# Low parts of streamed weights: a negated copy on ScalarE and an accumulating load, in place of VectorE's subtraction

## The chip, the core and the metric

One core of a Trainium2 chip runs the whole program. The metric is the device time of one execution in microseconds (us). TensorE multiplies matrices, VectorE and ScalarE work on elements, GpSimd does some element work and issues its own DMAs, and SyncE issues most of the loads. In the profile they are PE (with PEld for its weight loads), DVE, ACT, POOL and SP.

## The reference, cut to what matters

One layer of a diffusion backbone in float32: 512 latent tokens and 256 context tokens of width 1024. Every heavy step is a product of activations with a weight matrix that is used once.

```python
def swiglu(x, w_in, w_out):
    a, b = jnp.split(x @ w_in, 2, axis=-1)
    return (jax.nn.silu(a) * b) @ w_out
...
h = h + 0.5 * g1 * swiglu(modulate(h, norm_ffn1[layer], sh1, sc1), w_ffn1_in[layer], w_ffn1_out[layer])
hc = hc + 0.5 * g1c * swiglu(modulate(hc, norm_ffn1[layer], sh1c, sc1c), w_ffn1_in[layer], w_ffn1_out[layer])
...
q, k, v, rg, cv, ga, gb = jnp.split(u @ w_in[layer], IN_SPLITS, axis=-1)
o, _, _ = bidir_retention(q, k, v, log_gf, log_gb, rf, rb)
h = h + g2 * mixer_output(o, rg, cv, ga, gb, *branch_w)
h = h + 0.5 * g3 * swiglu(modulate(h, norm_ffn2[layer], sh3, sc3), w_ffn2_in[layer], w_ffn2_out[layer])
return rmsnorm(h, final_norm)
```

`modulate` is an RMS norm with a scale and a shift per channel; these come from a product of a conditioning vector with `w_mod`. `mixer_output` joins a four-head retention and a convolution of width 31 by sigmoid gates. The SwiGLU's inner width is 2816.

## The kernel before, in words

The activations lie with channels on the 128 partitions and tokens along the free dimension. TensorE multiplies in the type float32r, which holds fewer bits than float32, so each operand is held as two float32r parts: a high part (the value rounded) and a low part (what the rounding took away). A product of two such pairs takes three matmuls (`mm3`, L90 to L92): high times high, high times the activation's low part, and, last, the weight's low part times the activation's high part.

Weights are streamed in 248 units of 128 partitions by 1024 columns (896 in some of the SwiGLUs' second matrices). `unit` (L77 to L84) makes one: SyncE loads the raw float32 tile (L79), ScalarE copies it into a float32r tile `wh` (L81), and VectorE subtracts that from the raw tile into `wl` (L83). Raw tiles, `wh` and `wl` have four buffers each, so the cast of a unit waits until TensorE has read the unit four earlier for the last time. `units` makes two at a time. The raw buffers (tag `wraw`) also serve the 56 tiles of `w_mod` that are streamed beside the first SwiGLU (`mods`, L175 to L185), the distance tables of the heads (L549), and the reloads of the retention's partial sums in the gates' stage (L759 to L761).

The order of the stages: the first modulations and norms with the first products (`start`, to about 80 us), the first SwiGLU for latent and context tokens, keys, queries, values, scores and gates of four heads with the convolution's chunks between them (`retention`, `conv_chunk`), the gates of the two branches with the convolution's layernorm, the projection and the merge, and the second SwiGLU. A SwiGLU's last four units are held together, and their products are taken for the first half of the tokens and then for the second, so that the next norm can begin early; the merge's last products do the same.

A planner lists the instructions of each engine in one order, by priority and by the time at which it reckons them ready; on the chip each engine runs its list in that order, and a wait at the head holds up the rest. GpSimd's list holds, beside 16 products at the start (L164): the stores of h (L437), the zeroed margins of the convolution's input (L503, L504, with two buffers), the stores of the retention's partial sums (L718), their reloads (L761) and the reload of h (L788). The 30 taps of a convolution chunk (L515) run on VectorE at a lowered priority.

In the changed kernel the cast stands at L82, the negated copy at L84 and the accumulating load at L85, one line down for the rest of the function.

Of the kernel before, what the change touches and what calls it, by code (L numbers as in the profile page):

```python
# [16 lines left out]
P = 128  # L17
# [12 lines left out]
EPS = 1e-6  # L30
# [7 lines left out]
CONV_AT = ((0, 1, 2), (3, 4), (5, 6), (7,))  # L38
# The modulations that are computed beside the first SwiGLU: (which of the nine, channel block).
MOD_STEPS = (  # L40
# [9 lines left out]
def hybrid_layer_kernel(ctx: ExitStack, tc: tile.TileContext, a: dict, out: bass.AP):  # L50
# [21 lines left out]

# [1 line left out]
    def raw_tile(shape):  # L74
        return t_(shape, F32, "wraw", 4)

    def unit(src, n=1024):  # L77
        raw = raw_tile((P, n))
        nc.sync.dma_start(raw, src)  # L79
        hi = t_((P, n), F32R, "wh", 4)  # L80
        nc.scalar.copy(hi, raw)  # L81
        lo = t_((P, n), F32R, "wl", 4)  # L82
        nc.vector.tensor_sub(lo, raw, f32(hi))  # L83
        return hi, lo  # L84
# [12 lines left out]
    def proj(o, w, xs, ks=None, c=slice(None)):  # L97
        """o += w.T @ xs for the blocks ks of the contraction, all by default."""
        n = len(xs)
        for k in range(n) if ks is None else ks:  # L100
            mm3(o, col(w, k), (xs[k][0][:, c], xs[k][1][:, c]), k == 0, k == n - 1)

# [1 line left out]
    cs = cp.tile([P, KT, 2], F32, name="cs")  # L104
# [22 lines left out]
    nc.scalar.activation(cs, cs, AF.Silu)  # L127
    # the rows of c and c_ctx on every partition
    first = t_((P, P), F32, "sc")
# [15 lines left out]
    def first_mods(b):  # L145
        """The first scale and shift of channel block b. The engines share the work: the tensor engine finds
        the scales, the vector engine the latent tokens' shift, GpSimd (with ScalarE's sums) the context's."""
        raw = [[t_((P, 512), F32, rtags[(4 * b + 2 * i + n) % 24]) for n in range(2)] for i in range(2)]
        for i in range(2):
            for n in range(2):  # L150
                nc.sync.dma_start(raw[i][n], a["w_mod0"][2 * b + i, :, n * 512:(n + 1) * 512])
        pm = ps()
        for k in range(KT):
            nc.tensor.matmul(pm[0:2, 0:P], cs[:, k, :], raw[0][k // 4][:, k % 4 * P:(k % 4 + 1) * P],
                             start=k == 0, stop=k == KT - 1)
        row = tmp()
        nc.vector.tensor_copy(row[0:2, 0:P], pm[0:2, 0:P])
        nc.tensor.transpose(pm[:, P:P + 2], row[0:2, 0:P], ident[0:2, 0:2])
        for n in range(2):
            c = slice(n * 512, (n + 1) * 512)  # L160
            nc.vector.scalar_tensor_tensor(tmp((P, 512), BF16), raw[1][n], 1.0, ccrow[0][:, c], ALU.mult, ALU.mult,
                                           accum_out=dots[:, b, 0, n:n + 1])
            m = tmp()
            nc.gpsimd.tensor_mul(m, raw[1][n], ccrow[1][:, c])  # L164
            nc.scalar.activation(m, m, AF.Copy, accum_out=dots[:, b, 1, n:n + 1])
        nc.vector.tensor_scalar(ab1[:, 0, b, :], pm[:, P:P + 2], bm1[:, 8 + b:9 + b], vec[:, V_N1 + b:V_N1 + b + 1],
                                ALU.add, ALU.mult)
        shift(slice(b, b + 1), 0)
# [21 lines left out]
    def scale_shift(key, src, sc, sh, nrm, b, n=1):  # L190
        """The per-channel factor w * (1 + scale) and the shift of a modulated norm, n blocks from b."""
        if key not in deriv:
            deriv[key] = cp.tile([P, 2, 8], F32, name=f"ab_{key}")
        t = deriv[key][:, :, b:b + n]
        j = 8 * sc + b
        nc.vector.tensor_add(t[:, 0, :], src[:, j:j + n], bm1[:, j:j + n])
        nc.vector.tensor_mul(t[:, 0, :], t[:, 0, :], vec[:, nrm + b:nrm + b + n])
        j = 8 * sh + b
        nc.vector.tensor_add(t[:, 1, :], src[:, j:j + n], vec[:, V_BM + j:V_BM + j + n])
# [12 lines left out]

# [1 line left out]
    def square_sum(acc, src, b):  # L214
        """Adds the squares of block b to acc; those of the last block stay apart."""
        if b == 0:
            nc.scalar.activation(acc, src, AF.Square)
            return None
        sq = tmp()[:, :src.shape[-1]]
        if b == KT - 1:  # L220
            nc.vector.tensor_mul(sq, src, src)
            return sq
        nc.scalar.activation(sq, src, AF.Square)
        nc.vector.tensor_add(acc, acc, sq)

    def rstd_sum(acc, sq, c):
        """1 / sqrt(mean + eps) of acc's and sq's sum over the channels, a diagonal block for 128 tokens each."""
        n = c.stop - c.start
        nt = n // P
        pv = ps()  # L230
        for i in range(nt):
            o = pv[:, 2 * i:2 * i + 2]
            nc.tensor.matmul(o, acc[:, c.start + i * P:c.start + (i + 1) * P], ones[:, 0:2], start=True, stop=False)  # L233
            nc.tensor.matmul(o, sq[:, i * P:(i + 1) * P], ones[:, 0:2], start=False, stop=True)  # L234
        v = tmp((P, 2, 4))
        y = v[:, 1, :nt]
        rsqrt(y, v[:, 0, :nt], pv[:, 0:2 * nt:2], 1.0 / D)
        dg = tmp()
        for i in range(nt):
            nc.vector.tensor_scalar_mul(dg[:, i * P:(i + 1) * P], ident_h, y[:, i:i + 1])  # L240
        return dg[:, :n]

    def rstd_bcast(dg):
        """The same factors on every partition, in PSUM."""
        pr = ps()
# [7 lines left out]
    def rsqrt(y, var, src, scale):  # L253
        """y = -2 / sqrt(var), with var = scale * src + EPS: the table's root and one of Newton's steps."""
        n = y.shape[-1]
# [31 lines left out]

# [1 line left out]
    def ffn(w_in, w_out, u, uc, tags, evac, evac_c, extra, head, tail):  # L289
        """head gives the products of the first two chunks; tail is called between the products of the last  # L290
        four units, which take the first half of the tokens before the second."""
        g, gc = [], []
# [59 lines left out]

# [1 line left out]
    whole, wholec = slice(0, L), slice(0, LC)  # L354
    u, uc = u_tiles(), uc_tiles()

    def start():
        """The first modulations and norms, and the first two chunks' products as their inputs come."""
        for b in range(KT):
# [104 lines left out]

    # log decays of both directions: min(z, 0) - log1p(exp(-|z|))
    lg = cp.tile([P, 8], F32, name="lg")
# [16 lines left out]

# [1 line left out]
    uc, u = st["uc"], st["u"]  # L485
# [34 lines left out]
    def roped(p, half, hi, lo):  # L520
        """Rotation of a block whose partitions are (x1, x2), by angles that run with the grid's
        rows (half 0) or columns (half 1)."""
        if half == 0:
# [14 lines left out]
    def windows(strip, off, n):  # L538
        """Two windows of a strip, 128 apart."""
        w = strip[:, off:off + n]  # L540
        return bass.AP(w.tensor, w.offset, [list(w.ap[0]), [P, 2], [1, n]])

    def strips(hd):
        """Decays of all distances, latent keys and context keys, for one head."""
        gf, gb = lg[:, hd:hd + 1], lg[:, 4 + hd:5 + hd]
# [17 lines left out]
    def retention(hd):  # L563
# [35 lines left out]
        if hd == 0:  # L599
            # the norm of the latent tokens ends beside the first products  # L600
            w = units(a["w_k"][hd])
# [15 lines left out]
        def values():  # L617
            """Values, with tokens on the partitions."""
            pv = [ps() for _ in range(6)]
# [22 lines left out]

        # scores of six key blocks, times the decays, for half of the queries at a time
        for nh in range(2):
# [77 lines left out]

# [1 line left out]
    ret, gcv, z = [], [], []  # L724
# [48 lines left out]

# [1 line left out]
    mg = u_tiles()  # L775
# [37 lines left out]

# [1 line left out]
    acc3 = acc  # L815
# [41 lines left out]
def _constants():  # L857
# [5 lines left out]
    for pos in (rows, cols):  # L863
        ang = (inv[:, None] * pos[None, :]).astype(np.float32).astype(np.float64)
        c, s = np.cos(ang) * 0.25, np.sin(ang) * 0.25
        # the sine of a partition multiplies what moves to the other half
        parts += [np.concatenate([c, c]), np.concatenate([s, -s])]
# [9 lines left out]
def _layout(x, c, ctx, c_ctx, w_mod, b_mod, norm_ffn1, w_ffn1_in, w_ffn1_out, norm_mix, w_in, ret_decay_f,  # L877
# [5 lines left out]
    def square(w):  # L883
        # (K, N) -> pairs of column blocks: [N/256][P][2][K/128][128]
        k, n = w.shape
        return w.reshape(k // P, P, n // 256, 2, P).transpose(2, 1, 3, 0, 4).reshape(n // 256, P, -1)

    def halves(w):
        # column block i of the first half beside that of the second
        k, n = w.shape  # L890
# [61 lines left out]
```

## Time and profile before

| | |
|---|---|
| median of 2 runs | 1778.8 us (1778.37 to 1779.22) |
| the profiled execution, first to last instruction (span) | 1775.7 us |
| median above the span | 3.1 us |
| TensorE busy | 1749.0 us, 98% |
| VectorE busy | 1038.7 us, 58% |
| ScalarE busy | 575.1 us, 32% |
| GpSimd busy | 65.9 us, 4% |
| mean granted TensorE clock | 0.994 |
| moved by DMA | 199.95 MB, 113 GB/s over the span |

The profiled execution's own time is known as its span; the 3.1 us are the difference between that and the runs' median. A group of the profile reads: line, engine, operation, the tile written and those read, shapes, count, then busy us and mean ns of one, then the idle time just before and what ended it. TensorE's matmuls overlap: one of 512 columns is shown as some 370 to 400 ns long, but the next begins 0.23 us after it. "us to landing" is the time from a DMA's issue to its last byte.

### The profile page before, as it was taken

The numbers are of one execution on the slowest core, as the hardware profiler recorded it, in microseconds if no ns is written. First come the engines' busy times: TensorE is split into PE (matmuls) and PEld (weight loads), VectorE is DVE, ScalarE is ACT, GpSimd is POOL, SyncE is SP. The second block draws the span as 40 slices with busy tenths as digits, with TensorE's granted clock in tenths as the row PEclk, the third lists the DMA queues.
The fourth block names the chain that finished last, engine by engine and source line by source line (L and its number), as shares of the span: only waits on it lengthen the run. The fifth ranks groups of instructions, "written<-read, shape, count | busy, mean of one in ns | idle before, by whom it ended". The sixth has DMA issues, their size and how long they took to land. (4 is left out here: it accounts for less than half of the span.)

```text
span 1775.7 us, 22456 instructions
## 1 busy us (share of the span) xinstructions
PE 1749.0 (98%) x9182; PEld 1498.7 (84%) x9182; DVE 1038.7 (58%) x1646; ACT 575.1 (32%) x809; POOL 65.9 (4%) x111
## 2 busy tenths in 40 slices
PE   6999999999999999999999999999999999999997
PEld 4788888888889988888888888888888988888887
DVE  7755825452444798793876679293755643333335
ACT  5422113211222532432342334233562432222222
POOL 4100000000000000000000000001100000000000
PEclk8999999999999999999999999999999999999999
DMA  9133523362433321152142125114652133233321
GB/s 349 37 119 119 187 74 121 127 194 74 133 121 125 103 92 64 60 166 71 49 144 94 60 72 173 65 48 166 201 196 102 60 119 95 97 95 97 103 84 48
DMA packets 60156, 199.95 MB, mean 113 GB/s; under 512 B 7250, under 2 KB 7250, under 8 KB 60052
## 3 DMA queue, kind: packets, MB, share of 16 engines
q1 hardware_dynamic: 53140, 176.20, 29.8%
q0 software_dynamic: 6336, 21.25, 3.6%
q8 instruction: 72, 1.18, 0.3%
q10 hardware_dynamic: 576, 1.05, 0.2%
q14 instruction: 32, 0.26, 0.0%
HBM read 185.89 MB, written 12.58 MB: 112 GB/s over the span
## 5 line engine op out<-in xcount | busy, mean ns | idle before, releaser
L81 ACT CAST wh<-wraw 128x1024 fp32r<-128x1024 f32 (+1 forms) x248 | 257.2, 1038 | 640.3 <-PE ps L91 390.1
L83 DVE TENSOR_TENSOR wl<-wraw,wh 128x1024 fp32r<-128x1024 f32 (+1 forms) x248 | 298.5, 1206 | 255.9 <-ACT wh L81 251.7
L92 PE MATMUL ps<-uh,wl 128*128 128x512 f32 (+1 forms) x992 | 373.5, 377 | 2.2 <-DVE wl L83 2.2
L90 PE MATMUL ps<-uh,wh 128*128 128x512 f32 (+1 forms) x992 | 375.4, 380 | 0.3 <-ACT uh L270 0.3
L91 PE MATMUL ps<-ul,wh 128*128 128x512 f32 (+1 forms) x992 | 373.5, 377 | 0.0
L90 PE MATMUL ps<-gx,wh 128*128 128x512 f32 (+1 forms) x748 | 277.6, 373 | 0.2 <-ACT gx L278 0.2
L92 PE MATMUL ps<-gx,wl 128*128 128x512 f32 (+1 forms) x748 | 277.6, 372 | 0.0
L91 PE MATMUL ps<-gx,wh 128*128 128x512 f32 (+1 forms) x748 | 277.5, 372 | 0.0
L92 PEld LDWEIGHTS ps<-uh,wl 128*128 128x128 f32 x992 | 187.2, 189 | 37.2 <-DVE wl L83 2.9
L90 PEld LDWEIGHTS ps<-uh,wh 128*128 128x128 f32 x992 | 186.9, 189 | 34.7 <-issue 1.1
L91 PEld LDWEIGHTS ps<-ul,wh 128*128 128x128 f32 x992 | 187.3, 189 | 33.4 <-issue 0.5
L515 DVE SCALAR_TENSOR_TENSOR h<-y,vec,h 128x512 f32<-128x512 f32 x240 | 179.7, 749 | 5.4
L90 PEld LDWEIGHTS ps<-gx,wh 128*128 128x128 f32 x748 | 140.7, 188 | 24.6 <-ACT gx L278 0.4
L92 PEld LDWEIGHTS ps<-gx,wl 128*128 128x128 f32 x748 | 140.5, 188 | 24.6
L91 PEld LDWEIGHTS ps<-gx,wh 128*128 128x128 f32 x748 | 140.6, 188 | 24.0
L91 PE MATMUL ps<-uc,wh 128*128 128x256 f32 (+1 forms) x508 | 150.9, 298 | 0.2 <-DVE uc L271 0.2
L90 PE MATMUL ps<-uc,wh 128*128 128x256 f32 (+1 forms) x508 | 150.6, 297 | 0.3 <-ACT uc L270 0.3
L92 PE MATMUL ps<-uc,wl 128*128 128x256 f32 (+1 forms) x508 | 150.5, 297 | 0.0
L427 DVE SCALAR_TENSOR_TENSOR h<-ps,g_x,h 128x512 f32<-128x512 f32 (+1 forms) x68 | 44.6, 656 | 129.5 <-PE ps L92 129.2
L91 PE MATMUL ps<-gc,wh 128*128 128x256 f32 (+1 forms) x320 | 102.6, 321 | 0.0
L90 PE MATMUL ps<-gc,wh 128*128 128x256 f32 (+1 forms) x320 | 102.4, 320 | 0.0
L92 PE MATMUL ps<-gc,wl 128*128 128x256 f32 (+1 forms) x320 | 102.4, 320 | 0.0
(217 smaller groups left out, 2195.7 us busy)
## 6 DMA issues: line engine op xcount, KB each, us to landing
wraw<-in_w_mod SPq DMA_DIRECT2D x56, 512.0 KB, 3.5
wraw<-in_w1i SPq DMA_DIRECT2D x44, 512.0 KB, 3.8
wraw<-in_w2i SPq DMA_DIRECT2D x44, 512.0 KB, 3.7
wraw<-in_w_cv SPq DMA_DIRECT2D x16, 512.0 KB, 3.7
wraw<-in_w_v SPq DMA_DIRECT2D x16, 512.0 KB, 6.5
wraw<-in_w_rg SPq DMA_DIRECT2D x16, 512.0 KB, 3.6
wraw<-in_w_ro SPq DMA_DIRECT2D x16, 512.0 KB, 3.8
ypart<-t POOLq DMA_DIRECT2D x32, 256.0 KB, 4.3
```

The source lines that it names most:

```text
L81: nc.scalar.copy(hi, raw)
L83: nc.vector.tensor_sub(lo, raw, f32(hi))
L90: nc.tensor.matmul(o, w[0], x[0], start=first, stop=False)
L91: nc.tensor.matmul(o, w[0], x[1], start=False, stop=False)
L92: nc.tensor.matmul(o, w[1], x[0], start=False, stop=last)
L427: nc.vector.scalar_tensor_tensor(dst, p, g[:, b:b + 1], dst, ALU.mult, ALU.add)
L515: nc.vector.scalar_tensor_tensor(o, y[:, t:t + L], vec[:, w0 + t:w0 + t + 1], o, ALU.mult, ALU.add)
```

## The change

The low part is formed another way. ScalarE writes the negated raw tile, rounded to float32r, into the `wl` tile: minus the high part, since the rounding has no sign. Then GpSimd issues a DMA that reads the same weights once more from HBM and adds them to what stands in `wl`: the raw value minus the high part. VectorE has no part in it, and the raw tile is free once ScalarE has read it twice.

```diff
     def unit(src, n=1024):
         raw = raw_tile((P, n))
         nc.sync.dma_start(raw, src)
         hi = t_((P, n), F32R, "wh", 4)
         nc.scalar.copy(hi, raw)
         lo = t_((P, n), F32R, "wl", 4)
-        nc.vector.tensor_sub(lo, raw, f32(hi))
+        nc.scalar.activation(lo, raw, AF.Copy, scale=-1.0)
+        nc.gpsimd.dma_start(lo, src, accum_op=ALU.add)
         return hi, lo
```

The rest of the diff takes comments and docstrings out.

## The prediction

> **What bounds the kernel now.** I read the page first, then the busy time by stage, then who TensorE waits for.
>
> ```profile
> span 1775.7 us, 22456 instructions
> PE 1749.0 (98%) x9182; PEld 1498.7 (84%) x9182; DVE 1038.7 (58%) x1646; ACT 575.1 (32%) x809; POOL 65.9 (4%) x111
> L81 ACT CAST wh<-wraw 128x1024 fp32r<-128x1024 f32 (+1 forms) x248 | 257.2, 1038 | 640.3 <-PE ps L91 390.1
> L83 DVE TENSOR_TENSOR wl<-wraw,wh 128x1024 fp32r<-128x1024 f32 (+1 forms) x248 | 298.5, 1206 | 255.9 <-ACT wh L81 251.7
> ```
>
> TensorE is busy for 1749.0 of 1775.7 us, which leaves 26.7 us in which it isn't. The subtraction that the change removes (L83) is 298.5 us of VectorE, which at 58% is not the bound. By stage (columns: length, then busy us and count of PE, PEld, DVE, ACT, POOL, the granted clock, DMA share, GB/s):
>
> ```profile
> 0.00:80.00 80.00, 63.53 (x315) 43.06 (x316) 64.65 (x143) 39.42 (x81) 27.94 (x30) 0.91 0.56 201
> 80.00:600.00 520.00, 520.00 (x3082) 464.55 (x3082) 255.79 (x422) 119.49 (x178) 5.44 (x10) 1.00 0.38 123
> 1430.00:1745.00 315.00, 315.00 (x1399) 261.22 (x1398) 113.06 (x122) 85.05 (x104) 0.00 (x0) 1.00 0.29 91
> 1745.00:1776.00 31.00, 21.66 (x175) 20.87 (x173) 16.67 (x48) 4.41 (x10) 0.00 (x0) 0.90 0.19 69
> ```
>
> The holes are at the two ends: 16.5 us in the first 80, 9.3 us in the last 31; the 26.7 us leave 0.9 for all between. So removing VectorE work can win only at the start (the tail loads no weights), and any wait that the new chain adds after 80 us is added to the time in full. What TensorE waits for (total us, times, longest):
>
> ```profile
> PE ps L158 <- DVE t L157: 6.7, 4, 3.6
> PE ps L137 <- ACT wraw L134: 6.1, 1, 6.1
> PE ps L92 <- DVE wl L83: 2.2, 2, 1.7
> ```
>
> The low part of a weight unit is late twice in the whole run, for 2.2 us. The median of the two runs, 1778.8 us, is 3.1 us above the span; I add these 3.1 at the end.
>
> **What is added and removed.** Each of the 248 units loses 1.21 us of VectorE and gains a second ScalarE pass of the same form as L81 (1.04 us), a GpSimd issue and an accumulating load of up to 512 KB. Rows of the nearest operations (page, DMA issues: median us to landing; then GpSimd's groups, and the commonest VectorE instruction of the middle, for later):
>
> ```profile
> wraw<-in_w2i SPq DMA_DIRECT2D x44, 512.0 KB, 3.7
> ypart<-t POOLq DMA_DIRECT2D x32, 256.0 KB, 4.3
> wraw<-ypart POOLq DMA_DIRECT2D x16, 512.0 KB, 4.4
> L718 POOL DMA_DIRECT2D ypart<-t x32 | 17.2, 541 | 126.7 <-ACT t L717 126.7
> L761 POOL DMA_DIRECT2D wraw<-ypart x16 | 8.5, 532 | 180.8 <-DVE wl L83 141.6 <-DVE gx L770 23.8 <-DVE wraw L767 14.6
> ...
> L515 DVE SCALAR_TENSOR_TENSOR h<-y,vec,h 128x512 f32<-128x512 f32 x240 | 179.7, 749 | 5.4
> ```
>
> As sums these engines bear it: VectorE 1038.7 - 298.5 = 740 us; ScalarE 575.1 + 257 = 832; GpSimd 65.9 + 248 x 0.53 = 197. None comes near TensorE's 1749. The DMA engines carry another 248 x at most 0.52 MB = 130 MB; in the second SwiGLU, where all traffic is weights, a share of 0.29 becomes 0.58 if an accumulate costs what a load costs, and 0.87 if twice that. So throughput holds while an accumulate takes no more engine time than about 2.4 loads by the share (3.2 by bytes, with 386 GB/s of a full window, below, against 91).
>
> What matters is latency. Before, low parts were ready 1.2 us after the cast. After, the chain is: cast (L81), negated copy 1.04 us, about 0.1 for the two hand-overs, then X, the time from GpSimd's issue to the landing. The copy needs the raw tile alone and the slot that TensorE's last L92 frees, one matmul after the one that frees the slot of the high part, so it follows the cast at once; behind it on ScalarE wait the PSUM evacuations, 1 us later than now.
>
> No row shows an accumulate. Its lower bound is the plain GpSimd load of the same bytes into SBUF, 4.4 us. Its upper bound takes reading the old contents as separate transfers: 512 KB out of SBUF as two stores of 4.3, so 13.0 in all. The nearest row is the load (same queue, bytes and target); I add one more pass of 512 KB at the rate of the busy windows (386 GB/s, below): 1.3 us. **X = 5.7 us**, estimated from those rows. A gain over 4.4 is excluded, since the same bytes are fetched and something is added to them.
>
> Against that stands the cover of each unit: from the end of its cast to the first L92 that reads its low part. In the steady second SwiGLU and at the thinnest places:
>
> ```profile
> 1571.83 1.05 ACT L81 CAST wh<-wraw 128x1024 fp32r<-128x1024 f32 x1 [3.84 <-PE ps L91]
> 1588.59 0.39 PE L92 MATMUL ps<-gx,wl 128*128 128x512 f32 x1
> ...
> 79.80 1.05 ACT L81 CAST wh<-wraw 128x1024 fp32r<-128x1024 f32 x1 [0.70 <-PE ps L91]
> 86.42 0.39 PE L92 MATMUL ps<-uh,wl 128*128 128x512 f32 x1
> ...
> 1293.19 2.00 ACT L81 CAST wh<-wraw 128x1024 fp32r<-128x1024 f32 x2
> 1300.50 0.39 PE L92 MATMUL ps<-uh,wl 128*128 128x512 f32 x1
> ...
> 1418.03 1.05 ACT L81 CAST wh<-wraw 128x1024 fp32r<-128x1024 f32 x1 [1.16 <-PE ps L91]
> 1425.38 0.39 PE L92 MATMUL ps<-gx,wl 128*128 128x512 f32 x1
> ```
>
> Steady: 1588.59 - 1572.88 = 15.7 us, set by four buffers (the cast waits for the unit four earlier). It needs 1.15 + X = 6.85, so the steady stretches are safe. Where a stage ends with four units used by halves of the tokens, slots come free late: 86.42 - 80.85 = 5.6; 1300.50 - 1294.2 = 6.3 (first of the pair; the raw tile was late there); 1425.38 - 1419.08 = 6.3. I paired all 248 casts with their first L92 in the same way: after 80 us, 7 units have a cover under 6.9 us (5.6, 6.3, 6.3, 6.6, 6.7, 6.7, 6.8), 28 under 10.2, the rest more. A shortfall moves all that follows. Summed over the run, with later shortfalls counted only where they exceed the shift they inherit, the added wait is: X = 4.4: 0; 5.7: 2.8 (1.3 + 0.6 + 0.5 + 0.3 + 0.1); 7: 12; 9: 37; 10: 57; 12: 117; 13: 152 us. At X = 5.7 this term is **+2.8 us**.
>
> **The start.** Here VectorE and the DMA engines are full together:
>
> ```profile
> 30.00:35.00 5.00, 5.00 (x26) 2.93 (x24) 5.00 (x12) 2.88 (x6) 3.31 (x4) 0.78 1.06 386
> ...
> 22.64 1.21 DVE L83 TENSOR_TENSOR wl<-wraw,wh 128x1024 fp32r<-128x1024 f32 x1
> 24.91 1.21 DVE L83 TENSOR_TENSOR wl<-wraw,wh 128x1024 fp32r<-128x1024 f32 x1
> 26.04 0.73 DVE L269 SCALAR_TENSOR_TENSOR t<-h,ab,ps 128x512 f32<-128x512 f32 x1
> ...
> 37.74 1.03 ACT L81 CAST wh<-wraw 128x1024 fp32r<-128x1024 f32 x1
> 43.22 0.50 PE L92 MATMUL ps<-uh,wl 128*128 128x512 f32 x1 [1.73 <-DVE wl L83]
> 48.49 0.22 PE L158 MATMUL ps<-ident,t 2*128 2x2 f32 x1 [0.31 <-DVE t L157]
> 55.74 0.22 PE L158 MATMUL ps<-ident,t 2*128 2x2 f32 x1 [2.02 <-DVE t L157]
> ```
>
> Two subtractions stand ahead of the first norm (L269), so its chain comes 2.4 us earlier. The fourth unit pays: its cast, which follows that chain, ends at 38.77 - 2.4 = 36.4; copy and hand-over 1.15; and on full DMA engines two queues halve each other's rate, so both passes take twice 1.3 and X is 5.7 + 2.7 = 8.4. Its low part is there at 45.9, 2.7 us after the 43.22 of now. The waits of 0.31 and 2.02 that follow take up 2.3 of it. Start: **+0.4 us**. Bounds: a gain of all four subtractions, -4.8, if accumulates aren't slowed; +8 if X there is 13 and only those 2.3 us take it up. The second L83 wait of the run, 2.2 - 1.7 = 0.5 us, came from a busy VectorE and goes: **-0.5**.
>
> Sum: 1775.7 + 2.8 + 0.4 - 0.5 = 1778.4, plus 3.1 outside the span: **1781.5 us**; 1774 to 1791 over X from 4.4 to 7 and the start's likelier half.
>
> **The queues that are passed.** SyncE's loads of raw tiles now wait for ScalarE's copy in place of L83: about as late as before, so nothing. GpSimd runs in order: an accumulate waits there for its copy, and behind it wait the ypart stores, their reloads (L761), the memsets of y and the stores of h; in turn an accumulate stands behind those. The L761 row has 180.8 us of waiting before 16 issues: harmless now, with nothing behind it.
>
> A rule of the skill speaks against the move. The row first: under a VectorE that is busy for 58% of the span, 32 and 16 GpSimd issues took 541 and 532 ns on average. The Trainium skill, "SBUF — State Buffer", section "SBUF: two separate sides", says that GpSimd builds the descriptors of its DMAs itself and is locked out of a port shared with VectorE while VectorE runs in a two-port mode. No sign of it is in those issue rows, though they don't show when descriptors were written.
>
> **Rivals.**
>
> *The accumulate lands late.* If X is above 9 us, 28 thin places (stage ends, the first SwiGLU's units whose raw tiles come late at a cover of 9.9, the gates) each wait, TensorE has no other work, and the run is slower by 2% or more: 2% is 35.6 us, and 37 us is the price at X = 9; 117 at 12, to 1896. For it: adding must read, add and write, and nothing here shows how fast; the upper bound of 13 lies well beyond. Against it: a DMA-full window moves 386 GB/s, so plain passes of 512 KB are cheap beside the latency. Chance 0.25.
>
> *GpSimd's order holds it up.* In the gates' stage reloads (L761) wait for tiles; an accumulate behind one waits with it. At 8 pairs and 3 us each: +24, to 1806. The trace shows L761 released by wl (141.6 of 180.8 us), a release that comes no later after the change. Chance 0.05.
>
> *GpSimd is locked out by VectorE.* If each issue waits for one VectorE instruction of the kind that fills most of the busy middle (0.75 us, L515), X is 6.5 and the sum over the places 7.6 in place of 2.8: 1786. By the rule named above such waits would exist. Chance 0.04, for the even issue rows.
>
> *The lighter VectorE wins at the start.* X = 4.4 there and elsewhere: -4.8 - 0.5, to 1773.5. Chance 0.06. More than 2% can't be had from waits: all holes together are 26.7 us, below 35.6. 0.01 is for a cause that I don't see.
>
> **How the numbers follow.** The forecast has 0.59. It, the three small rivals (0.05, 0.04, 0.06) lie within 2%, which is about what a measurement of this kernel can tell from no change: 0.74. Slower by over 2% is the late accumulate: 0.25. Faster: 0.01. The range begins at 1772, under the gain; upward it takes in the late accumulate to X = 10.5 (+70): 1850, which leaves out about 0.15 above and 0.03 below.
>
> **What would show it.** Right: L83's groups gone, ScalarE near 832 us, VectorE near 740, TensorE's waits on wl few and short, landings of the accumulating loads of 5 to 7 us, and no new hole between 80 and 1745 us of more than 2 us. Wrong: landings above 9 us or a DMA share near 1 in the second SwiGLU; then TensorE waits for the load at each stage's end, and above 14 us in each unit of that stage too.

## The result and the profile after

The changed kernel takes 1884.72 us (two runs, 1882.26 and 1887.19) against 1778.8: slower by a factor of 1.0598, 95% interval 1.0563 to 1.0633. The forecast was 1781.5, the range ended at 1850; the case that came true is the late accumulate, which had a chance of 0.25, and it came at a higher price than the range allowed.

The page of the changed kernel (lines are one or two further down: cast L82, negated copy L84, accumulating load L85, matmuls L92 to L94):

```profile
span 1885.3 us, 22908 instructions
PE 1787.5 (95%) x9182; PEld 1518.0 (81%) x9182; DVE 761.6 (40%) x1398; ACT 799.2 (42%) x1055; POOL 279.7 (15%) x359
...
PEclk8899999999999989999999999999989999999999
...
q0 software_dynamic: 42048, 149.20, 40.3%
...
L84 ACT ACTIVATE wl<-wraw 128x1024 fp32r<-128x1024 f32 (+1 forms) x248 | 258.2, 1041 | 76.1 <-PE ps L93 76.1
...
wl<-in_w1i POOLq DMA_DIRECT2D x44, 512.0 KB, 9.3
wraw<-in_w2i SPq DMA_DIRECT2D x44, 512.0 KB, 6.6
wl<-in_w2i POOLq DMA_DIRECT2D x44, 512.0 KB, 7.8
```

The subtraction is gone and no engine is overloaded. The span grew by 1885.3 - 1775.7 = 109.6 us, in two parts: TensorE stands idle for 1885.3 - 1787.5 = 97.8 us where it was 26.7, which is 71.1 more; and the same 9182 matmuls take 1787.5 us instead of 1749.0, which is 38.5 more. By stage up to 1745 us (columns as in the prediction: PE, PEld, DVE, ACT, POOL, clock, DMA share, GB/s):

```profile
0.00:80.00 80.00, 64.42 (x306) 41.93 (x306) 58.55 (x138) 42.84 (x84) 26.66 (x34) 0.89 0.69 227
80.00:600.00 520.00, 510.68 (x2958) 451.32 (x2959) 172.53 (x333) 173.21 (x230) 58.85 (x69) 0.99 0.72 184
600.00:1262.00 662.00, 635.13 (x3178) 539.66 (x3177) 382.48 (x658) 299.08 (x386) 89.42 (x125) 0.98 0.62 147
1262.00:1560.00 298.00, 261.02 (x1265) 220.00 (x1264) 90.45 (x167) 150.73 (x194) 55.84 (x75) 0.93 0.79 196
1560.00:1745.00 185.00, 185.00 (x818) 153.19 (x817) 24.93 (x35) 79.17 (x92) 29.73 (x34) 1.00 0.87 191
```

The steady second SwiGLU (last row) has no hole, as forecast. The loss lies in the first SwiGLU (9.3 us idle), the heads (26.9) and most densely from the gates to the second SwiGLU's first chunks (37.0 idle in 298, at a clock of 0.93). The start cost 1.2 us: the 315th product, which ends it, begins at 81.3 us instead of 80.1. What TensorE waits for there:

```profile
PE ps L94 <- DMA wl<-in_w_gab: 18.5, 5, 6.6
PE ps L94 <- DMA wl<-in_w_k: 17.0, 5, 5.7
PE ps L94 <- DMA wl<-in_w1i: 10.5, 7, 3.5
PE ps L94 <- DMA wl<-in_w2i: 8.3, 4, 3.9
PE ps L94 <- DMA wl<-in_w_cv: 6.7, 2, 5.4
...
PE ps L94 <- DMA wl<-in_w_co: 5.8, 1, 5.8
```

All waits on low parts come to 71.4 us in 30 times, by the accumulating load's own line (`PE ps L94` among those who waited for it), which also has its time to landing:

```profile
  PE ps L94: 71.4, 30
...
DMA to landing us min/median/max: 5.2/8.0/13.0
```

X, which I put at 5.7, is 8.0 in the median, 5.2 to 13.0. One of the waits, at the first key unit of a head, in order of time, and then the stretches of the wait and of what follows it:

```profile
813.14 0.39 PE L93 MATMUL ps<-ul,wh 128*128 128x512 f32 x1
818.50 0.79 PE L94 MATMUL ps<-uh,wl 128*128 128x512 f32 x1 [4.98 <-DMA wl<-in_w_k]
819.10 0.63 PE L92 MATMUL ps<-uh,wh 128*128 128x512 f32 x1
819.52 0.63 PE L93 MATMUL ps<-ul,wh 128*128 128x512 f32 x1
...
825.65 0.40 PE L92 MATMUL ps<-uh,wh 128*128 128x512 f32 x1
```

```profile
813.50:818.40 4.90, 0.03 (x1) 0.00 (x0) 4.14 (x7) 2.58 (x3) 0.86 (x1) 0.91 1.05 278
818.50:824.40 5.90, 5.89 (x14) 4.64 (x15) 2.08 (x4) 2.52 (x3) 0.86 (x1) 0.51 1.00 243
```

After the wait the matmuls begin 0.43 us apart instead of 0.23, for about 6 us, at a granted clock of 0.51. So a wait is paid twice. The clock's records show such half-clock periods of 3.41 us each, one to three behind a wait: 4 before the tail in the kernel before, 28 in this one. The 24 more, at half speed, are 24 x 3.41 / 2 = 41 us, which answers to the 38.5 us of longer busy time. The prediction had no term for this.

### The profile page after: what moved, and what is told of

The parts are those of the page before. It is cut to its first block, busy times and chain, and to the rows that moved or that the text cites. A ratio compares the mean times of both kernels' runs of the same rounds, so it can differ in the third digit from the quotient of the medians.

```text
span 1885.3 us, 22908 instructions
## 1 busy us (share of the span) xinstructions
PE 1787.5 (95%) x9182; PEld 1518.0 (81%) x9182; DVE 761.6 (40%) x1398; ACT 799.2 (42%) x1055; POOL 279.7 (15%) x359
## 3 DMA queue, kind: packets, MB, share of 16 engines
q0 software_dynamic: 42048, 149.20, 40.3%
q10 hardware_dynamic: 576, 1.05, 0.1%
## 5 line engine op out<-in xcount | busy, mean ns | idle before, releaser
L82 ACT CAST wh<-wraw 128x1024 fp32r<-128x1024 f32 (+1 forms) x248 | 256.6, 1035 | 501.6 <-issue 236.7
L94 PE MATMUL ps<-uh,wl 128*128 128x512 f32 (+1 forms) x992 | 385.5, 389 | 54.1 <-DMA wl<-in_w_gab 18.5
L92 PE MATMUL ps<-uh,wh 128*128 128x512 f32 (+1 forms) x992 | 383.6, 388 | 1.3 <-ACT uh L272 1.1
L93 PE MATMUL ps<-ul,wh 128*128 128x512 f32 (+1 forms) x992 | 380.6, 384 | 0.1
L94 PE MATMUL ps<-gx,wl 128*128 128x512 f32 (+1 forms) x748 | 281.3, 377 | 14.2 <-DMA wl<-in_w2i 8.3
L84 ACT ACTIVATE wl<-wraw 128x1024 fp32r<-128x1024 f32 (+1 forms) x248 | 258.2, 1041 | 76.1 <-PE ps L93 76.1
L92 PE MATMUL ps<-gx,wh 128*128 128x512 f32 (+1 forms) x748 | 280.7, 377 | 1.1 <-ACT gx L280 1.1
L93 PE MATMUL ps<-gx,wh 128*128 128x512 f32 (+1 forms) x748 | 280.5, 376 | 0.0
L94 PEld LDWEIGHTS ps<-uh,wl 128*128 128x128 f32 x992 | 192.2, 194 | 99.5 <-DMA wl<-in_w_gab 20.6
L92 PEld LDWEIGHTS ps<-uh,wh 128*128 128x128 f32 x992 | 192.5, 195 | 37.7 <-ACT uh L272 2.0
L93 PEld LDWEIGHTS ps<-ul,wh 128*128 128x128 f32 x992 | 192.0, 194 | 35.7 <-DVE ul L273 0.5
L94 PEld LDWEIGHTS ps<-gx,wl 128*128 128x128 f32 x748 | 142.9, 192 | 40.9 <-DMA wl<-in_w2i 9.5
L299 DVE TENSOR_TENSOR t<-t,ps 128x512 f32<-128x512 f32 x44 | 30.2, 687 | 341.2 <-PE ps L94 337.0
L92 PEld LDWEIGHTS ps<-gx,wh 128*128 128x128 f32 x748 | 142.8, 191 | 25.7 <-ACT gx L280 1.3
L93 PEld LDWEIGHTS ps<-gx,wh 128*128 128x128 f32 x748 | 142.9, 192 | 24.6
L94 PE MATMUL ps<-uc,wl 128*128 128x256 f32 (+1 forms) x508 | 150.7, 298 | 0.9 <-DMA wl<-in_w_k 0.9
L92 PE MATMUL ps<-uc,wh 128*128 128x256 f32 (+1 forms) x508 | 150.6, 297 | 0.3 <-ACT uc L272 0.3
L94 PE MATMUL ps<-gc,wl 128*128 128x256 f32 (+1 forms) x320 | 102.8, 321 | 2.2 <-DMA wl<-in_w1o 2.2
L92 PE MATMUL ps<-gc,wh 128*128 128x256 f32 (+1 forms) x320 | 102.7, 321 | 0.0
```

The source lines that it names most:

```text
L84: nc.scalar.activation(lo, raw, AF.Copy, scale=-1.0)
L92: nc.tensor.matmul(o, w[0], x[0], start=first, stop=False)
L93: nc.tensor.matmul(o, w[0], x[1], start=False, stop=False)
L94: nc.tensor.matmul(o, w[1], x[0], start=False, stop=last)
L299: nc.vector.tensor_mul(s, s, pb)
```

## The experiments

The runs ask two things: what makes low parts late, and whether the half clock is a cost of its own. The kernel before took 1778.4 to 1779.1 us beside these runs. The diffs are against the kernel after unless they say otherwise. Where no interval stands, a kernel was run once. The two runs of the kernel after lie 4.9 us apart and most repeats of the kernel before between 1775.1 and 1782.9, so a difference under some 8 us, alone, says little.

**The accumulate left out.**

```diff
         nc.scalar.activation(lo, raw, AF.Copy, scale=-1.0)
-        nc.gpsimd.dma_start(lo, src, accum_op=ALU.add)
```

> The accumulating load is left out, so the low parts hold the negated weights and the output is another one; ScalarE's negated copy stays. Theory (the loads land late, some 8 us after issue where 5.7 were reckoned with; waits over about 3.5 us then halve the granted clock for 3.4 to 10 us; in the gates' stage GpSimd's order adds to it): without the load all of the 106 us go, 1775 to 1785 us, clock 0.99. Rival A (ScalarE's second pass holds up other work on ScalarE and with it TensorE): a good part stays, above 1810 us.

1772.97 us.

```profile
span 1771.2 us, 22392 instructions
PE 1746.8 (99%) x9182; PEld 1496.8 (85%) x9182; DVE 760.4 (43%) x1398; ACT 797.9 (45%) x1055; POOL 62.5 (4%) x111
```

ScalarE's second pass costs nothing that can be seen. Without any subtraction this one run is 6 us below the kernel before, and 5.5 of them are gained in the start (the 250th product begins at 63.4 us instead of 68.9). The load costs 1884.7 - 1773.0 = 112 us.

**A plain load in its place**, which leaves the addition out.

```diff
-        nc.gpsimd.dma_start(lo, src, accum_op=ALU.add)
+        nc.gpsimd.dma_start(lo, src)
```

> GpSimd's load is a plain one of the same bytes to the same place at the same point of its list, so the addition is left out and the output is another one. Theory: landings fall from 8 us to 5 to 6, most thin places are covered, 1785 to 1815 us; what stays is in the gates' stage (GpSimd's order). Rival B (it is the issue from GpSimd and its order, not the addition): landings stay near 8 us and the time above 1860 us.

1813.19 us, span 1811.3. Its DMA queue of GpSimd's transfers and its time to landing:

```profile
q0 software_dynamic: 42048, 149.20, 23.9%
...
DMA to landing us min/median/max: 3.6/5.0/11.8
```

A plain load of the same bytes on the same path already costs 40 us over the run without a load; the addition costs the other 72. The same 149.20 MB in GpSimd's queue take 23.9% of 1811.3 us on the DMA engines as plain loads and 40.3% of 1885.3 as accumulates. The kernel before has 3.6% of 1775.7 in this queue for its other transfers; without them it is 369 and 696 us, a factor of 1.9 for the same bytes. The Trainium skill, "Collectives: The Full Stack", section "The bandwidth ceiling: the fold count and why AG ≠ RS ≠ AR", says of another kind of transfer that a reduction emits two source reads for each chunk where a copy emits one, and is slower for the second read, not for the adding. The factor of 1.9 agrees with two passes for one; no run here shows the reads themselves.

**Two accumulates of half the size.**

```diff
-        nc.gpsimd.dma_start(lo, src, accum_op=ALU.add)
+        for c in (slice(0, n // 2), slice(n // 2, n)):
+            nc.gpsimd.dma_start(lo[:, c], src[:, c], accum_op=ALU.add)
```

> Each accumulating load is cut into two of half the columns; the first matmuls of a unit need the first half alone. Theory: the first half lands about 2 us sooner than the whole, so waits shorten by as much at each thin place and some fall below the length that halves the clock: 1835 to 1870 us. Rival C (DMA throughput or GpSimd's issue time, 0.87 us each, now twice): no better than 1885 us, landings of the halves as late as those of the whole.

1858.33 us: 26 us less, with landings of 3.9/7.1/13.6 us and GpSimd busy for 504 us. The first half of a unit is what TensorE reads first, so part of the landing is hidden. That it helps speaks for the landing as a cause and against the number of issues.

**VectorE makes the negated copy.**

```diff
-        nc.scalar.activation(lo, raw, AF.Copy, scale=-1.0)
+        nc.vector.tensor_scalar_mul(lo, raw, -1.0)
```

> The negated copy is made by VectorE in place of ScalarE; the accumulating load stays. Theory: the landings are as before, 1865 to 1890 us. Rival A (ScalarE's second pass comes late in ScalarE's list, by up to 7 us at the heads' keys): the waits there shorten, below 1850 us.

1876.06 us, 9 less. The copy's engine matters little. The waits on the keys' units stayed (15.9 us instead of 17.0), for on VectorE the copy (818.90) stands behind the product of the decay strips, which waits for an exponential of ScalarE; what holds that one up is shown further down:

```profile
816.44 1.09 DVE L556 TENSOR_TENSOR sx<-sx,wraw 128x896 f32<-128x896 f32 x1 [3.74 <-ACT wraw L555]
...
818.90 0.69 DVE L84 TENSOR_SCALAR wl<-wraw 128x1024 fp32r<-128x1024 f32 x1
```

GpSimd's issues now stretch further than in the kernel after (860 to 1297 ns in all groups):

```profile
L85 POOL DMA_DIRECT2D wl<-in_w_cv x16: 863/872/2262, 672.1 to 1185.5; - x16
L85 POOL DMA_DIRECT2D wl<-in_w_q x8: 859/1242/1491, 625.2 to 1123.0; - x8
```

**Low parts last.** In each projection all products with high parts are issued first, then those with the weight's low part, so that the first low part is wanted by the 17th product instead of the third. With eight blocks that is 14 products of 0.227 us, 3.2 us later (the expectation below says 15). The same edit was made in the kernel before.

```diff
-        for k in range(n) if ks is None else ks:
-            mm3(o, col(w, k), (xs[k][0][:, c], xs[k][1][:, c]), k == 0, k == n - 1)
+        ks = list(range(n) if ks is None else ks)
+        for k in ks:
+            x, hi = xs[k], col(w, k)[0]
+            nc.tensor.matmul(o, hi, x[0][:, c], start=k == 0, stop=False)
+            nc.tensor.matmul(o, hi, x[1][:, c], start=False, stop=False)
+        for k in ks:
+            nc.tensor.matmul(o, col(w, k)[1], xs[k][0][:, c], start=False, stop=k == n - 1)
```

> The changed kernel; in each projection all products with the weights' high parts come first and those with their low parts last, so that the first low part is needed 15 matmuls later (3.4 us at 512 columns, 1.7 at 256). Theory (landing against cover): most waits of projections fall away, 1790 to 1825 us; what stays is at the halves and behind GpSimd's order in the gates. Rival C (throughput): near 1885 us.

> The kernel before with the same order of products as in the run with low parts last. Theory: its two waits for a low part (2.2 us) go and nothing else changes: 1775 to 1780 us. Rival: the order itself costs or gains more than 5 us, and the run with the changed kernel must be read against this one.

1833.72 us for the changed kernel, 51 less than as it was; 1783.03 for the kernel before, 4.7 more. The landing is as it was (5.3/7.9/13.2), so half of the loss goes by wanting the low part later alone (51 us are left over the kernel before with the same order). The first expectation was missed by 9 us: waits of 12.1 us on the gates' units and 8.0 on the keys' stay. The second was missed by 3: the kernel before kept its two waits on low parts (2.4 us).

**SyncE issues the reloads of ypart**, which in the gates' stage stand ahead of accumulates in GpSimd's order. In the kernel after, on GpSimd:

```profile
1282.04 0.53 POOL L763 DMA_DIRECT2D wraw<-ypart  x1 [8.04 <-DVE wraw L769]
...
1284.37 1.85 POOL L85 DMA_DIRECT2D wl<-in_w_gab  x2
```

The copy for the first of these two accumulates had ended at 1276.5 (L84 at 1275.43, 1.08 us): 7.9 us lost behind a reload that waits for a tile and three stores behind that reload, where an accumulate follows its copy after 0.3 us in the median.

```diff
-            nc.gpsimd.dma_start(yp[i], ypart[:, m, 2 * i:2 * i + 2, :])
+            nc.sync.dma_start(yp[i], ypart[:, m, 2 * i:2 * i + 2, :])
```

> The changed kernel, with the reloads of the partial sums in the gates' stage issued by SyncE in place of GpSimd. Theory: the accumulating loads of that stage no longer stand 5 to 11 us behind a reload that waits for its tile; three waits of 4 to 6 us and their slow periods go, 25 us in all, to about 1860 us. Rival: the raw tiles are what is short there, SyncE's own loads now stand behind the reloads, and the stage is no faster.

1876.86 us: 8 less, not 25. The gates' waits went from 18.5 to 13.9 us, and the wait on the layer norm (at 1352.0 in the kernel after, 1343.7 here) from 2.9 to 7.7. The order was real, but it was not the only thing late: in the kernel after, the longest of the gates' waits (6.6 us, at 1383.52) belongs to an accumulate that was issued 0.3 us behind its copy. There the raw tile came late, and the copy then stood 7.6 us behind its cast, after other activations and three loads of ScalarE's tables (1.28 us each):

```profile
1367.99 1.05 ACT L82 CAST wh<-wraw 128x1024 fp32r<-128x1024 f32 x1 [4.70 <-DMA wraw<-in_w_gab]
...
1376.61 1.06 ACT L84 ACTIVATE wl<-wraw 128x1024 fp32r<-128x1024 f32 x1
```

**A ladder of delays in the kernel before.** Six subtractions of the second SwiGLU were repeated 15 to 23 times, to make TensorE wait without any accumulate.

```diff
-        nc.vector.tensor_sub(lo, raw, f32(hi))
+        for _ in range(reps):
+            nc.vector.tensor_sub(lo, raw, f32(hi))
```

> The kernel before, with the subtraction of one unit repeated 15, 16, 17, 18, 20 and 23 times at six places of the steady second SwiGLU, so that TensorE waits there for about 1, 2, 4, 5, 7 and 10 us beside idle DMA queues; nothing else changes. Theory (a wait over about 3.5 us halves the granted clock): after the short waits the clock stays at 1.00, after the long ones it is 0.50 for one to three periods of 3.4 us, and the span grows by the waits (about 29 us) and by half of the slow periods (some 10 us more). Rival D (the half clock in the changed kernel comes from DMA load or from power): the span grows by the waits alone, and the clock stays at 1.00 at all six.

1783.04 us; inconclusive. TensorE waited 0.5 us for low parts in all, so the run says nothing on the clock. I take it that the planner, which reckons with the delays, put other products in their place; that isn't shown.

**Waits filled with useless products.** At the eleven low parts for which the kernel after waits over 3 us, the unit's first product is issued again 16 to 30 times ahead of the wait.

```diff
+            if k == 0:
+                us = pend.pop(w[0].tensor.name, 0.0)
+                x0 = xs[0][0][:, c]
+                for _ in range(round(us / 0.227 * 512 / x0.shape[-1])):
+                    nc.tensor.matmul(o, col(w, 0)[0], x0, start=True, stop=True)
             mm3(o, col(w, k), ...)
```

> The kernel after, with 264 extra products of TensorE in front of the eleven low parts for which it waited over 3 us: the first product of that unit (high part, first block) is issued again 16 to 30 times, about as long as the wait was, 56 us in all; each restarts the same sum, so the result stays. If the half clock follows TensorE's own standing still, the waits become useless work, nothing is lost by that, and the half-clock periods behind those places go: about 22 of 26 added ones, each worth 3.41 us / 2, so 37 us: 1845 to 1860 us, granted clock 0.99. If the half clock comes from anything else (the traffic, the late loads), the time stays at 1880 to 1890. If the waits were not where I put the products, the 56 us are added: 1940.

1874.49 us: 264 more products, and 10 us less time.

```profile
span 1872.5 us, 23432 instructions
PE 1816.9 (97%) x9446; PEld 1546.3 (83%) x9446; DVE 764.8 (41%) x1398; ACT 798.9 (43%) x1055; POOL 280.7 (15%) x359
```

```profile
785.00:816.10 31.10, 30.85 (x136) 25.23 (x135) 23.44 (x33) 18.91 (x24) 9.07 (x15) 1.00 0.82 218
```

The window holds the same key unit's filled wait and stays at clock 1.00. Of 28 half-clock periods 8 are left before the tail. The added products are 232 of 0.227 us and 32 of 0.117, 56.4 in all, so the kernel's own took 1816.9 - 56.4 = 1760.5 us, 27 less than the 1787.5 of the kernel after: the half clock came from TensorE's standing still, not from the traffic or the late loads. (There were 24 added periods, not the 26 that the expectation counted.) The time missed the expectation by 14 us because the other part didn't hold: the idle time and the fill together are 55.6 + 56.4 = 112, where the idle time alone had been 97.8. I read it so: where TensorE no longer crawled after a wait, the next low part was late by more, for a wait of 7.4 us stood at the convolution's first unit (5.4 before) and one of 6.9 at the layer norm (2.9 before). So the half clock had hidden waits, and its price is not 41 us that could be had back by themselves; some 10 of them could.

**The subtraction kept where the cover is thin.** For 32 units (the first four, and those whose cover in the kernel before is under 10.2 us) VectorE subtracts as before; 216 units accumulate. A second kernel keeps it for 64 units, those under 13 us.

```diff
-        nc.scalar.activation(lo, raw, AF.Copy, scale=-1.0)
-        nc.gpsimd.dma_start(lo, src, accum_op=ALU.add)
+        if made[0] in SUB:
+            nc.vector.tensor_sub(lo, raw, f32(hi))
+        else:
+            nc.scalar.activation(lo, raw, AF.Copy, scale=-1.0)
+            nc.gpsimd.dma_start(lo, src, accum_op=ALU.add)
```

> The kernel after, with VectorE's subtraction kept for the 32 units whose cover in the kernel before is under 10.2 us (and the first four); the other 216 low parts are formed by copy and accumulate. If cover against the accumulate's landing decides alone, nothing waits over 3 us and it takes 1778 to 1786 us. If the order of ScalarE's and GpSimd's queues adds to it, the first key unit of three heads and the first gates' unit, whose covers of 11.3 to 11.6 are left with the accumulate, still wait 5 to 6 us each, with half a period to a period and a half of half clock behind: 1800 to 1820. If the doubled traffic slows all loads, over 1825.

> The same with the subtraction kept for the 64 units of a cover under 13 us, and the accumulate for 184. By cover, with or without the queues' order: 1776 to 1784 us, no wait for a low part over 2 us, granted clock 0.994 as before. If the traffic or the number of GpSimd's issues is what costs, still over 1800, since three quarters of them stay.

1839.45 us for the first, 1786.51 for the second (ratio to before 1.0043, interval 1.0029 to 1.0057). The first one's waits, and then the second one's page and its only wait on an accumulate of note:

```profile
PE ps L101 <- DMA wl<-in_w_k: 16.2, 3, 6.4
PE ps L101 <- DMA wl<-in_w_gab: 12.3, 4, 6.1
PE ps L256 <- DVE t L249: 8.8, 3, 5.9
```

```profile
PE 1752.7 (98%) x9182; PEld 1499.1 (84%) x9182; DVE 832.5 (47%) x1462; ACT 743.0 (42%) x993; POOL 227.7 (13%) x295
...
PE ps L101 <- DMA wl<-in_w_co: 2.8, 1, 2.8
```

Three quarters of the accumulates, with a median landing of 7.8 us, cost 7.4 us (against the 1779.1 beside them), 2.5 above the expected range. So neither the traffic as a whole nor the number of issues is what costs; it is what happens at the thin places. (The 64 subtractions also take their loads out of those places; the run doesn't part the two.) But the 32 units between 10.2 and 13 us cost 53 us, which landing against cover doesn't explain (8.0 + 1.15 = 9.2): the expectation from cover alone fell, by 53 us, the one with the queues' order was 20 too low, and by its number the run falls under the third, slower loads. The next run asks which of the last two it is.

**The exponentials taken out of ScalarE's way.** At the first key unit of a head in the kernel after, and at the same place in the kernel before (ScalarE, in order of time):

```profile
797.59 1.05 ACT L554 ACTIVATE sx<-wraw,lg 128x896 f32<-128x896 f32 x1 [1.74 <-DMA wraw<-in_dist_x]
804.03 1.04 ACT L555 ACTIVATE wraw<-wraw,lg 128x896 f32<-128x896 f32 x1 [5.40 <-DMA wraw<-in_dist_x]
...
807.83 1.09 ACT L84 ACTIVATE wl<-wraw 128x1024 fp32r<-128x1024 f32 x1
```

```profile
770.38 1.04 ACT L553 ACTIVATE wraw<-wraw,lg 128x896 f32<-128x896 f32 x1 [0.71 <-DMA wraw<-in_dist_x]
```

An exponential that makes the decay strips waits for a distance load. SyncE issued that load at 794.58 and it released ScalarE at 804.03, 9.4 us later; in the kernel before it was 766.12 to 770.38, 4.3 us. The same stretch, from issue to exponential in the second to fourth head, took 3.8 to 4.3 us in the kernel before, 4.1 to 5.3 with the load left out, 7.0 to 7.6 with plain loads and 9.3 to 9.4 with accumulates: the second loads of the weights are what slows it. Cast and copy stand behind it, so the copy began 7.6 us after its buffer was free at 800.2 (the end of the last product that read it). This run is the one with 32 subtractions kept, and the first head's strips serve all four heads, which leaves the other heads' distance loads and exponentials out:

```diff
+        if kept:
+            return kept[0]
         gf, gb = lg[:, hd:hd + 1], lg[:, 4 + hd:5 + hd]
...
+        kept.append((sx, sc))
         return sx, sc
```

> The kernel with the subtraction kept at 32 thin units (1839.45 us), and the decay strips of the first head used for all four: the distance loads and the exponentials of three heads are left out, so the result is another. There TensorE waited 16.2 us for the first key unit's low part of three heads, and six half-clock periods stood behind (6 x 3.41 / 2 = 10 us). If ScalarE's copy was late because an exponential ahead of it in order waited for its distances, these 26 us go: 1810 to 1818 us, waits on the keys' low parts under 2 us. If the accumulate is late there by its own landing (the engines are 80% busy), the waits stay: 1835 to 1840.

1820.18 us: 19 less than 1839.45, and no wait on a key unit is left in its list; the first row of that list is

```profile
PE ps L101 <- DMA wl<-in_w_gab: 8.1, 4, 5.8
```

So both were needed: a load that the accumulates' traffic had slowed, and ScalarE's order behind it. (The three heads' distance loads also no longer take raw buffers; the run doesn't part that, but the rows above name the load.) It came out 2 us above the expected range.

**And SyncE for the reloads as well.**

The edit is that of the reloads above, made in the kernel with one strip.

> The same, and SyncE issues the reloads of ypart in the gates' stage instead of GpSimd. TensorE waited there 12.3 us for the gates' low parts and 6.1 for the layer norm (L256), with five half-clock periods behind (8.5 us). If GpSimd's order is what holds up those accumulates, about 18 us less than the kernel with one strip: 1793 to 1800. If it is the tiles' release and the landing, or if the reloads now hold up SyncE's raw loads, within 8 us of it.

1817.11 us, 3 less, which two single runs can't tell from nothing: GpSimd's order alone isn't what holds the gates' stage. There waits of 10.2 us on the gates' low parts and 5.6 on the layer norm stay. What is late first in that stage wasn't settled; the layer norm's matmul waits for VectorE, and ScalarE waits for raw loads between its casts. The 31 us between this run and the one with 64 subtractions have not been divided up.

**The start alone.** Two edits of the kernel before, for its first two units: copy and accumulate; and, second, the subtraction on GpSimd.

```diff
+        made[0] += 1
+        if made[0] <= 2:
+            nc.scalar.activation(lo, raw, AF.Copy, scale=-1.0)
+            nc.gpsimd.dma_start(lo, src, accum_op=ALU.add)
+        else:
+            nc.vector.tensor_sub(lo, raw, f32(hi))
-        nc.vector.tensor_sub(lo, raw, f32(hi))
```

```diff
+        made[0] += 1
-        nc.vector.tensor_sub(lo, raw, f32(hi))
+        (nc.gpsimd if made[0] <= 2 else nc.vector).tensor_sub(lo, raw, f32(hi))
```

> The kernel before, with copy and accumulate for the first two of the 248 units alone, where two subtractions stand ahead of the first norm on VectorE. The accumulates were issued at 18.6 and 21.1 us and first read at 28.2 and 30.1. If the two subtractions hold up the start and the landing of up to 9 us fits: 1775.5 to 1777.5 us, 1.3 to 3.3 below the kernel before. If the accumulates land late beside the inputs' loads: 1779 or more.

> The kernel before, with the first two subtractions on GpSimd instead of VectorE, no accumulate at all. If the two subtractions on VectorE hold up the first norm, 1775 to 1777.5 us; if the copies to the first two units with accumulate gained nothing because the start is bound elsewhere (VectorE's later work, the inputs' loads), 1778 to 1779.5 again; over 1780 if GpSimd's pass is longer than 5 us or stalls VectorE.

1777.82 us (ratio 0.9996, interval 0.9987 to 1.0005) and 1779.84 (1.0009, 1.0000 to 1.0018): neither differs from the kernel before by what can be told. With the accumulates the first norm began at 24.21 instead of 26.04 us, and it made no difference at the end that these runs can resolve. With GpSimd's subtraction VectorE lost the gain ahead of it. Of four instructions (here and in the kernel before) one took 2.38 us, to the end of GpSimd's subtraction, and one 1.30, to the end of the product that GpSimd makes next:

```profile
16.86 4.00 DVE L243 TENSOR_SCALAR t<-ident_h,t 128x128 f32<-128x128 f32 x4
```

```profile
17.91 0.88 DVE L240 TENSOR_SCALAR t<-ident_h,t 128x128 f32<-128x128 f32 x4
```

No version that computes the whole reference came out faster than the kernel before.

## Why the prediction was wrong

Its frame held: TensorE is the bound, every wait after 80 us is added to the time, and sums of busy time don't decide. ScalarE was put at 832 us and is 799 (instructions back to back overlap by some 0.1 us), VectorE at 740 and is 762. GpSimd was put at 197 and is 280, for an accumulate's issue takes 873 ns in the median, not 530; a plain load on the same path took 528. The start was put at +0.4 us and cost 1.2. In the steady second SwiGLU the DMA share is 0.87, the value given for an accumulate that costs two loads, and no hole opened at a cover of 15.7 us, as said. What failed, by its own steps:

1. **X = 5.7 us** was mis-sized. It measured 8.0 (5.2 to 13.0; the 30 that TensorE waited for, 9.1 in the median), because I priced the addition as one pass more on free engines: 1.3 us, where the plain load's 5.0 against 8.0 makes it 3.0. The bounds 4.4 and 13.0 held, the upper one by chance: with VectorE's copy a landing took 16.7. By the prediction's own table an X of 8 is worth between 12 (X = 7) and 37 us (X = 9), so this step explains a third of the loss at most.

2. **"It follows the cast at once"**, of the copy, and its counterpart, the issue 0.1 us behind the copy, were taken from the steady stretch and used everywhere. At the heads' keys the copy came 7.6 us late, behind an exponential that waited for a load; at the gates the issue came 7.9 us late, behind a reload. The covers were measured rightly, but the chain that stood against them wasn't one length: from the cast's end to the landing, put at 6.85 us, it was 9.6 in the median, over 12.7 for a tenth of the units and 21.2 at most. The strongest sign is the plain load: at its 5.0 us the table gives under 3 us of added wait, and it lost 40. Waits on the keys' and gates' units are 17.0 + 18.5 = 35.5 of the 71.4 us; the other half lies at thin places of the kind that the table lists.

3. **"So throughput holds"** was argued from a stage's mean. It held there, but in bursts the engines are full (share 1.05 in the wait at 813.5), and then other loads are late too: the distance load at 9.4 us instead of 4.3, raw tiles of the second SwiGLU at 6.6 instead of 3.7. I had used such a full window for the start only.

4. **A shortfall was priced at its own length.** Each longer wait cost half clock behind it besides: 38.5 us of the 109.6, of which filling the waits gave 10 back. The rows that I had quoted showed it, with clocks of 0.78 and 0.91 in the start, and I read them as the start's affair. The Trainium skill states the rule, "TensorE: Matmul & The Clock Gate", section "Part 1: The HAM clock gate": after an idle window of about 3.4 us the clock is halved, and it takes a busy window of that length to release it. The trace agrees with the half rate and with the 3.41 us; how short a wait sufficed here stands at the end.

The rivals: **the late accumulate** was right in mechanism, and its 37 us at X = 9 fell short by steps 2 and 4. **GpSimd's order** was there (7.9 us at the gates), but taking it away gave 8 and 3 us. **Locked out by VectorE** doesn't show in this kernel, whose issues took 873 ns in the median and 1297 at most; issues of up to 2262 ns came when VectorE made the copy, but of up to 2002 ns also with ScalarE's copy and the loads halved, so that VectorE was the reason is not shown. **The lighter VectorE wins** is seen only without the load, in one run, for 6 us; the part that I put down to the first two subtractions (2.4 us) couldn't be told from nothing.

## What to carry to other kernels

A transfer put in place of an instruction must be held against the cover at the thinnest places, stage by stage, with the chain as it is there: what stands ahead of each of its links on that link's in-order engine, and how full the DMA engines are in that window rather than on average. A wait of TensorE of more than 2 to 3 us costs more than its length, since half clock follows it, though part of that price is hidden where the next operand would have been late anyway. Where only the wide covers were used (184 of 248 units) the trade cost 0.4% and gained nothing.

## What the runs showed of the hardware

- An accumulating load of 512 KB into SBUF landed after 8.0 us in the median against 5.0 for a plain one on the same queue, and took 1.9 times the DMA engines' time for the same bytes. Its issue took GpSimd 873 ns against 528.
- Over all traces of this case, after 80 us and before the tail, TensorE had 141 gaps over 1.2 us between matmuls, a gap being counted from 0.23 us after the start of a matmul of 512 columns, in proportion for fewer. Of the 50 shorter than 1.9 us none was followed by half clock, of the 29 from 1.9 to 3.0 us 18 were, of the 62 longer ones 60. The section of the Trainium skill cited above ("TensorE: Matmul & The Clock Gate", "Part 1: The HAM clock gate") speaks of an idle window of about 3.4 us; here shorter waits did it too. One is the wait of the kernel with 64 subtractions that the profile puts at 2.8 us, in two stretches, the wait's and the next:

```profile
1325.00:1329.00 4.00, 1.19 (x5) 0.67 (x4) 2.67 (x4) 2.75 (x4) 1.74 (x2) 1.00 1.02 264
1329.50:1332.90 3.40, 3.40 (x10) 2.66 (x9) 0.00 (x0) 0.00 (x0) 0.00 (x0) 0.50 1.05 271
```

- Useless matmuls in the place of waits made the kernel faster (1884.7 to 1874.5 us).
- While GpSimd subtracted (2.35 us, a 128 x 1024 tile), a VectorE instruction on 128 x 128 elements beside it took 2.38 us instead of 0.28.
